# A depthwise convolution's taps: more scaled by ScalarE and summed in pairs by accumulating transfers, in buffers that attention has left

## The chip, the cores and the metric

The kernel runs on one core of one Trainium2 chip. The metric is device time in microseconds of one execution; three runs of the kernel before took 1874.3, 1874.67 and 1877.3 us. The engines are TensorE (PE, matrix products; PEld is its loading of weights), VectorE (DVE), ScalarE (ACT), GpSimd (POOL) and SyncE (SP). POOL and SP here mostly issue transfers.

## The reference

Two layers of one mixer each over a sequence of 256 with 2048 channels. One input projection feeds a convolution branch (with a depthwise causal convolution of 31 taps and a layer norm over the channels) and an attention branch of 16 heads; gates merge them.

```python
def conv_branch(a, glu, gate, conv_w, conv_b, ln_g, ln_b):
    u = a * jax.nn.sigmoid(glu)
    u = lax.conv_general_dilated(u, conv_w[:, None, :], window_strides=(1,),
        padding=[(CONV_WIDTH - 1, 0)], feature_group_count=CONV_DIM) + conv_b
    u = jax.nn.silu(layernorm(u, ln_g, ln_b))
    return u * jax.nn.silu(gate)

def hybrid_layer(...):
    proj = rmsnorm(x, norm_g) @ w_in
    ...
    y_conv = conv_branch(c_a, c_glu, c_gate, ...) @ w_proj_conv
    y_mla = mla_branch(q_down, kv_down, k_pe, m_gate, ...) @ w_proj_mla
    y = jax.nn.sigmoid(g_conv) * y_conv + jax.nn.sigmoid(g_mla) * y_mla
    return x + y @ w_out
```

## The kernel before

All large products read weights from HBM in *pieces* of 128 rows by two blocks of (mostly) 512 columns, 512 KB each, which SP loads in the order of the products, four pieces ahead, into five `raw` buffers. Precision is kept by splitting: ACT rounds a piece to `hi` (three pieces ahead, four buffers), DVE makes `lo = raw - hi` (two pieces ahead, three buffers), and PE multiplies hi by hi, lo by hi and hi by lo for both halves of the sequence: 12 matmuls a piece. The products of a layer follow in the order `glu` (the convolution's input), `down`, then for eight pairs of heads `uq`, `ukv` and more `glu` and `cgate`, then `cgate`, `mgate`, `gmla`, `pmla`, `gconv`, `pconv` (the convolution branch's projection, whose stationary operand is `ycT`, a quarter of it for each two pieces of its first block) and `wout`.

Every engine's instructions run in the order in which the program records them. That order is drawn at recording time by a planner with a clock of one *slot* a piece: `product` records a piece's splits and matmuls and then calls `background`, which records

- the steps that are due at this slot (`at_slot`), attention's above all,
- work from the queue `fill` while a budget of DVE's time for this slot lasts: taps of the convolution, then the steps of the layer norm,
- calls of `assist` while ACT's budget lasts: ACT scales a tap ahead of DVE into a `wide` buffer, at most two ahead,
- and what was put off in `late`.

The convolution is worked on for eight blocks of 256 channels (`conv(b)`): `u` holds the block's input, `v_t` its sum, and a tap is two instructions of DVE (`scalar_tensor_tensor`, one for each 128 channels), or two of ACT and one add of DVE. A block's sum goes into `s1`. After the eighth block, `layernorm` puts its steps into `fill`: the mean over channels by a matmul (`mu`), centring and squares, a second matmul (`var`), the root by steps of DVE (`rsqrt_steps`), `apply` (times the root, then silu on ACT), `gated` (times the transposed gate) and `separated` (hi by ACT and lo by DVE into `ycT`). Before the first block of `pconv`, at each second piece, `before_pconv` draws from `fill` whatever is still missing for the next quarter of `ycT`.

The profile names all these instructions by the line of one helper, L136, which records them; the tiles' names tell them apart. In the names `acc` is a product's PSUM tile, `hT` and `h_hi`, `h_lo` the normalised input, `su` and `gate` gates that are transposed by way of HBM (`turn_d`, fetched as `turned`), `qk` an attention pair's queries and keys.

Work2's two `qk` buffers, of 1536 numbers a partition, belong to the pairs of heads in turn; behind the last pair one of them becomes `ln_stats`.

Of the kernel before, what the change touches and what calls it, by code (L numbers as in the profile page):

```python
# [25 lines left out]
CONV_W = 31  # L26
PAD = CONV_W - 1
# [8 lines left out]
NPAIR = N_HEADS // 2  # L36
# [4 lines left out]
EPS = 1e-6  # L41
# [83 lines left out]
def trunk(ctx: ExitStack, tc: tile.TileContext, xT, x, g_in, pos, win, wuq, wukv, wpc, wpm, wo, cst, rows, invf, out):  # L125
# [114 lines left out]


    steps, clock, late, early = [], [0], [], []
    fill, budget, marks, owed, assist = deque(), {"vec": 0.0, "act": 0.0}, {}, [], []
# [331 lines left out]
    for l in range(DEPTH):  # L575
# [199 lines left out]
        def attention(b, pair_of=pair_of, ss_d=ss_d, kpe=kpe, ccq=ccq, ssq_t=ssq_t, gqk=gqk, A=A):  # L775
# [95 lines left out]
            def maxima():  # L871
                s0, s1 = st["s"]
                sx = work.tile([P, 2, P], F32, tag="sx", name="sx")
                act.copy(sx, s0[:, :, 1, :])
# [48 lines left out]
            def outputs():  # L923
                o = A.o_sb[:, 2 * b : 2 * b + 2, :]
                act.copy(o, st["o"][:, :, 0, :])
                late.append(lambda: vec.tensor_add(o, st["o"][:, :, 1, :], o))
                A.pairs.pop(b)

            def later(ahead, *args, **kw):
                at_slot(ahead + PAIR_LATER[b], *args, **kw)  # L930
# [14 lines left out]


        us, vs, keep = {}, {}, {"separated": {}}
        s1 = layer_c.tile([P, 2, SEQ], F32, tag="s1c", name="s1c")

        def glu_evac(b, t, ps, us=us):  # L950
# [13 lines left out]
            early.append(product_out)  # L964

        def conv(b, us=us, vs=vs, s1=s1, C=C):
            scaled = {}
# [5 lines left out]
            def scale(k):  # L973

                while k in scaled:
                    k += 1
                if k == CONV_W or len(scaled) == 2:
                    return False
                scaled[k] = wide_p.tile([P, 2, SEQ], F32, tag="w", name="tap")
                for j in range(2):  # L980
                    act.activation(scaled[k][:, j, :], us[b][:, j, k : k + SEQ], AF.Copy, scale=weight(k, j))
                return True

            def tap(k):

                if k == 0:
                    vs[b] = uv_p.tile([P, 2, PAD + SEQ], F32, tag="uv", name="v_t")
                u, v, costs = us[b], vs[b], (0.81, 0.0)
                if k == 0:
                    for j in range(2):  # L990
                        bias = C[:, C_CB + 2 * b + j : C_CB + 2 * b + j + 1]
                        vec.tensor_scalar(v[:, j, :SEQ], u[:, j, :SEQ], weight(k, j), bias, op0=ALU.mult, op1=ALU.add)
                elif k in scaled:
                    vec.tensor_add(v[:, :, :SEQ], v[:, :, :SEQ], scaled.pop(k))
                    costs = (0.73, 0.0)
                else:
                    for j in range(2):
                        vec.scalar_tensor_tensor(
                            v[:, j, :SEQ], u[:, j, k : k + SEQ], weight(k, j), v[:, j, :SEQ], op0=ALU.mult, op1=ALU.add
                        )  # L1000
                assist[:] = [lambda: scale(k + 1)]
                if k == CONV_W - 1:
                    mark(("s1", b))
                    assist.clear()
                    if b == 0:
                        vec.tensor_copy(s1, v[:, :, :SEQ])
                    else:
                        vec.tensor_add(s1, s1, v[:, :, :SEQ])
                    costs = (costs[0] + 0.6, costs[1])
                    us.pop(b)  # L1010
                return costs

            for k in range(CONV_W):
                fill.append((lambda k=k: tap(k), (None, 0, False)))

        def layernorm(vs=vs, s1=s1, C=C, keep=keep):
            marks.clear()
            stats = work2.tile([P, 5, SEQ], F32, tag="qk", name="ln_stats")
            mu_sb, ms, rstd = (stats[:, i] for i in range(3))
            s2 = stats[:, 3:]  # L1020
            wide = lambda a: a.unsqueeze(1).broadcast_to([P, 2, SEQ])

            st = {}

            def mean():
                st["mu"] = tp_p.tile([P, SEQ], F32, tag="tp", name="mu")
                over_channels(st["mu"])
                mark("mean")

            def centre(b):  # L1030
                if b == 0:
# [25 lines left out]

            def whole_s2():
                finish_late()
                halves(s2)  # L1060
                mark("s2")
                return 1.1, 0.0

# [8 lines left out]
                mark("var")  # L1072

            def factors():
                vec.tensor_scalar(ms, st["var"], EPS, None, op0=ALU.add)
                st["rsqrt"] = rsqrt_steps(rstd, ms)
                next(st["rsqrt"])
                return 0.9, 0.0

# [3 lines left out]

            def apply(b):
                v = vs[b][:, :, :SEQ]
                vec.tensor_mul(v, v, wide(rstd))
# [373 lines left out]
```

## Time and profile before

| | |
|---|---|
| median of three runs | 1874.67 us |
| the profiled execution, its own time | 1874.78 us |
| its span, first to last instruction | 1873.0 us |
| mean granted PE clock | 0.982 |
| the chain that ended last | PE 92%, DVE 4%, ACT 2% |
| DVE, `lo` of 128x1024, x630 | 766.0 us, 1.22 us each |
| ACT, `hi` of 128x1024, x630 | 654.6 us, 1.05 us each |
| weights by SP's queue | 59.1% of the 16 DMA engines' span |
| transfers of POOL's queue | 13.5% |

A row of a group gives the engine, the operation, what it writes and reads with sizes, how many, the busy time in us, the mean of one in ns, and the idle time of the engine just before with what ended it. A row of the order of time gives the start and the duration in us. A row of waits gives the sum in us, how many and the longest. A row of stretches gives each engine's busy time in a stretch, PE's granted clock, the share of the DMA engines and GB/s.

### The profile page before, as it was taken

To read this page: it belongs to the slowest core of one execution; us is meant where nothing else is said; L and a number is where in the kernel's file an instruction comes from. 1 tells how busy PE (TensorE), PEld (TensorE's weight loads), DVE (VectorE), ACT (ScalarE), POOL (GpSimd) and SP (SyncE) were. 2 spreads that over 40 slices of the span, in tenths; PEclk is the share of its full clock that TensorE was granted. 3 is DMA by queue.
4 is the path that set the end of the run, shared out by engine and by line. 5 is a ranking of instruction groups with operands and counts; after the bars stand their busy time and mean duration, and the time that the engine had idled before them with its cause. 6 is when DMAs were issued, how large, how long until landed. Compare 5 with 4: busy or idle time off the path is not lost.

```text
span 1873.0 us, 27021 instructions
## 1 busy us (share of the span) xinstructions
PE 1803.1 (96%) x8577; PEld 1587.0 (85%) x8577; DVE 1587.8 (85%) x2526; ACT 1295.7 (69%) x2363; POOL 492.7 (26%) x942
## 2 busy tenths in 40 slices
PE   9999999999999995599999999999999999976999
PEld 9988888888888884488899888888888888865888
DVE  6898988899999998567679999889999999875664
ACT  7678889888766764445557688898887667553442
POOL 1155555543100000022320555555431000001210
PEclk9999999999999998799999999999999999988999
DMA  9788788888766664277977888888877666753785
GB/s 331 238 272 280 259 279 266 262 265 259 241 204 202 203 214 140 95 235 258 320 266 218 270 282 266 273 260 261 273 256 244 204 203 203 215 180 108 256 271 173
DMA packets 138959, 445.04 MB, mean 238 GB/s; under 512 B 23680, under 2 KB 29312, under 8 KB 138816
## 3 DMA queue, kind: packets, MB, share of 16 engines
q1 hardware_dynamic: 105120, 359.89, 59.1%
q0 software_dynamic: 32832, 82.62, 13.5%
q8 instruction: 67, 1.10, 0.2%
q10 hardware_dynamic: 864, 0.80, 0.1%
q14 instruction: 76, 0.62, 0.1%
HBM read 399.18 MB, written 44.04 MB: 237 GB/s over the span
## 4 chain that ended last, share of the span: by engine, by line
PE 92%; DVE 4%; ACT 2%; DMA 1%; POOL 1%; issue 1%; DVEq 0%; SPq 0%; ACTq 0%; POOLq 0%
PE acc L136 90%; PE s L136 1%; DVE v_t L136 1%; PE o_ps L136 1%; DVE lo L136 1%; ACT hi L136 1%; DVE ln_stats L136 1%; POOL rsq_t L136 0%; DVE turned L136 0%; DVE rsq_t L136 0%; DMA raw<-in_win 0%; ACT ycT L136 0%; ACT L136 0%; DMA gx<-in_g 0%; POOL turn_d L136 0%
## 5 line engine op out<-in xcount | busy, mean ns | idle before, releaser
L136 ACT CAST hi<-raw 128x1024 fp32r<-128x1024 f32 (+3 forms) x682 | 695.0, 1027 | 437.6 <-PE acc L136 374.4
L136 DVE TENSOR_TENSOR lo<-raw,hi 128x1024 fp32r<-128x1024 f32 (+3 forms) x682 | 812.1, 1193 | 182.3 <-PE acc L136 143.8
L136 PE MATMUL acc<-hi,hT 128*128 128x512 f32 (+2 forms) x1728 | 401.1, 372 | 0.9 <-ACT junk L136 0.5
L136 PEld LDWEIGHTS acc<-hi,hT 128*128 128x128 f32 x1728 | 319.5, 189 | 42.3 <-ACT junk L136 1.1
L136 PE MATMUL acc<-hi,h_hi 128*128 128x512 f32 (+2 forms) x864 | 251.9, 373 | 0.4 <-ACT hi L136 0.4
L136 PE MATMUL acc<-hi,h_lo 128*128 128x512 f32 (+2 forms) x864 | 251.4, 373 | 0.0
L136 DVE SCALAR_TENSOR_TENSOR v_t<-u_t,cst,v_t 128x256 f32<-128x256 f32 x564 | 242.9, 479 | 4.5
L136 PE MATMUL acc<-lo,h_hi 128*128 128x512 f32 (+2 forms) x864 | 220.5, 372 | 0.0
L136 PE MATMUL acc<-lo,hT 128*128 128x512 f32 (+2 forms) x864 | 220.2, 372 | 0.0
L136 POOL DMA_DIRECT2D turned<-turn_d x88 | 49.2, 559 | 602.6 <-DVE v_t L136 393.3
L136 PE MATMUL acc<-hi,ycT 128*128 128x512 f32 x512 | 137.5, 414 | 51.4 <-ACT ycT L136 51.4
L136 PEld LDWEIGHTS acc<-hi,h_lo 128*128 128x128 f32 x864 | 161.9, 189 | 20.8
L136 ACT ACTIVATE tap<-u_t,cst 128x256 f32<-128x256 f32 x396 | 179.0, 499 | 0.3 <-DVE v_t L136 0.3
L136 PEld LDWEIGHTS acc<-lo,h_hi 128*128 128x128 f32 x864 | 161.0, 189 | 20.7
L136 PEld LDWEIGHTS acc<-hi,h_hi 128*128 128x128 f32 x864 | 160.7, 189 | 20.9 <-ACT hi L136 0.8
L136 PEld LDWEIGHTS acc<-lo,hT 128*128 128x128 f32 x864 | 160.8, 189 | 20.6
L136 POOL DMA_DIRECT2D turn_d<-gate x184 | 100.0, 551 | 264.2 <-DVE gate L136 162.7
L136 PEld LDWEIGHTS acc<-hi,ycT 128*128 128x128 f32 x512 | 105.7, 208 | 72.1 <-ACT ycT L136 54.5
L136 DVE TENSOR_TENSOR v_t<-v_t,tap 128x512 f32<-128x512 f32 x198 | 135.5, 685 | 1.5 <-DVE v_t L136 0.5
L136 PE MATMUL acc<-hi,oT 128*128 128x512 f32 x512 | 122.2, 379 | 0.0
L136 PE MATMUL acc<-hi,yT 128*128 128x512 f32 x512 | 122.2, 378 | 0.0
L136 PE MATMUL acc<-hi,qkc 128*128 128x512 f32 x448 | 110.4, 379 | 0.0
(176 smaller groups left out, 2222.2 us busy)
## 6 DMA issues: line engine op xcount, KB each, us to landing
raw<-in_win SPq DMA_DIRECT2D x382, 512.0 KB, 4.4
raw<-in_wpm SPq DMA_DIRECT2D x64, 512.0 KB, 4.3
raw<-in_wpc SPq DMA_DIRECT2D x64, 512.0 KB, 3.8
raw<-in_wo SPq DMA_DIRECT2D x64, 512.0 KB, 5.0
raw<-in_wukv SPq DMA_DIRECT2D x32, 512.0 KB, 4.3
turned<-turn_d POOLq DMA_DIRECT2D x56, 256.0 KB, 5.0
raw<-in_win SPq DMA_DIRECT2D x32, 384.0 KB, 4.7
raw<-in_wuq SPq DMA_DIRECT2D x24, 512.0 KB, 4.4
```

The lines of the kernel that those rows point to most:

```text
L136: ins = getattr(self.engine, name)(*a, **k)
```

## The change

Behind the last pair of heads (`outputs` of the last pair calls `more_taps`), the two `qk` buffers become six buffers of a tap each (`spare`), and ACT's rule is changed from (0.8, 0.85) to (0.4, 1.1): it may go on at a smaller rest of its budget, and each tap is charged with more. `scale` now takes taps from the far end (`todo.pop()`), DVE from the near end. While `spare` has a buffer, ACT scales a tap into it; the second of two is added onto the first by a transfer that POOL issues with an accumulating write (`dma_start(whole, tap, accum_op=add)`). Three slots on, the second buffer is free again and DVE's `step` may add the sum of both, once, to `v_t`. Without `spare` all is as before, with at most two single taps ahead. The end of a block is a step of its own. In `maxima` the second half of the queries comes first: its mask and maximum stand before the add of the first half, which waits for a copy of ACT. `ln_stats` is allocated when the mean is recorded.

```diff
+MERGED_AT = 3
+BESIDE_PAIRS, BEHIND_PAIRS = (0.8, 0.85), (0.4, 1.1)
...
-        while assist and budget["act"] > 0.8 and assist[0]():
-            budget["act"] -= 0.85
+        while assist and budget["act"] > pace[0][0] and assist[0]():
+            budget["act"] -= pace[0][1]
...
             def maxima():
...
-                vec.tensor_add(sx, s0[:, :, 0, :], sx)
-                for s, nkeys in ((sx, P), (s1, SEQ)):
-
+                for t, (s, nkeys) in ((1, (s1, SEQ)), (0, (sx, P))):
+                    if t == 0:
+                        vec.tensor_add(sx, s0[:, :, 0, :], sx)
                     vec.memset(s[:CHUNK, :, nkeys - CHUNK :], MASKED)
-                nb = small.tile([P, T, 2], F32, tag="nb", name="nb")
-                vec.tensor_reduce(nb[:, 0], sx, axis=AX.X, op=ALU.max, negate=True)
-                vec.tensor_reduce(nb[:, 1], s1, axis=AX.X, op=ALU.max, negate=True)
+                    vec.tensor_reduce(nb[:, t], s, axis=AX.X, op=ALU.max, negate=True)
...
         def conv(b, us=us, vs=vs, s1=s1, C=C):
+            todo, singles, st = deque(range(1, CONV_W)), deque(), {"first": None}
...
+            def scale():
+
+                if len(todo) < 2:
+                    return False
+                merged = bool(spare)
+                if not merged and len(singles) == 2:
+                    return False
+                k = todo.pop()
+                tap = spare.popleft() if merged else wide_p.tile([P, 2, SEQ], F32, tag="w", name="tap")
                 for j in range(2):
+                    act.activation(tap[:, j, :], us[b][:, j, k : k + SEQ], AF.Copy, scale=weight(k, j))
+                if not merged:
+                    singles.append((clock[0] + 1, tap))
+                elif st["first"] is None:
+                    st["first"] = tap
+                else:
+                    whole, st["first"] = st["first"], None
+                    late.append(lambda: gps.dma_start(whole, tap, accum_op=ALU.add))
+                    merging.append((clock[0] + MERGED_AT, b, whole))
+                    at_slot(MERGED_AT, lambda: spare.append(tap))
                 return True
...
+            def step():
+
+                if merging and merging[0][0] <= clock[0]:
+                    return add_merged()
+                if singles and (singles[0][0] <= clock[0] or not todo):
+                    return add(singles.popleft()[1])
+                if todo:
+                    k = todo.popleft()
...
+                        vec.scalar_tensor_tensor(v, us[b][:, j, k : k + SEQ], weight(k, j), v, op0=ALU.mult, op1=ALU.add)
+                    return 0.81, 0.0
...
+        def more_taps():
+            pace[0] = BEHIND_PAIRS
+            for _ in range(2):
+                a = work2.tile([P, 3, 2, SEQ], F32, tag="qk", name="taps")
+                spare.extend(a[:, i] for i in range(3))
```

How the instructions stand now is seen on three places. First DVE in the first layer, around the first quarter of `ycT`. `lo` rows split the pieces, `ln_stats` holds the mean, the squares' sum and the root, `v_t<-v_t,ln_stats` is centring and later `apply`, `v_t<-turned,v_t` is the gate. Before:

```order
L136 TENSOR_TENSOR lo_7757<-raw_7662,hi_7741 128x1024
L136 COPY ln_stats<-mu 128x256
L136 TENSOR_TENSOR v_t<-v_t,ln_stats 128x2x256 x8
...
L136 TENSOR_TENSOR v_t<-v_t,ln_stats 128x2x256 x4
L136 TENSOR_TENSOR v_t<-turned,v_t 128x2x128 x2
L136 TENSOR_TENSOR lo_7853<-raw_7683,hi_7759 128x1024
L136 TENSOR_TENSOR v_t<-turned,v_t 128x2x128 x2
L136 TENSOR_TENSOR ycT_7848<-v_t,ycT_7847 128x512 x2
...
L136 TENSOR_TENSOR lo_7901<-raw_7725,hi_7885 128x1024
L136 TENSOR_TENSOR v_t<-v_t,ln_stats 128x2x256 x2
```

And now, the same place:

```order
L139 SCALAR_TENSOR_TENSOR ln_stats<-rsq_t,ln_stats 128x256
L139 TENSOR_TENSOR v_t<-v_t,ln_stats 128x2x256
L139 TENSOR_TENSOR lo_7691<-raw_7584,hi_7671 128x1024
L139 TENSOR_TENSOR v_t<-v_t,ln_stats 128x2x256 x2
L139 TENSOR_TENSOR lo_7713<-raw_7604,hi_7693 128x1024
L139 TENSOR_TENSOR lo_7735<-raw_7627,hi_7715 128x1024
L139 TENSOR_TENSOR v_t<-v_t,ln_stats 128x2x256
L139 TENSOR_TENSOR v_t<-turned,v_t 128x2x128 x4
L139 TENSOR_TENSOR lo_7764<-raw_7652,hi_7737 128x1024
L139 TENSOR_TENSOR ycT_7759<-v_t,ycT_7758 128x512 x2
...
L139 TENSOR_TENSOR lo_7828<-raw_7717,hi_7812 128x1024
L139 TENSOR_TENSOR v_t<-v_t,ln_stats 128x2x256 x2
```

Before, everything from the mean to the root stood between two `lo` rows, ahead of the first quarter; now it is spread over the `lo` rows of 17 pieces ahead, of which the last are seen. From `lo_7828` on (two `lo` rows are left out ahead of it) the rows of the second, third and fourth quarter stand in the same places as before, from `lo_7901` on there.

Second, DVE in the second layer, where `ycT`'s quarters are made; the `lo` rows stand for the last pieces of `gconv`:

```order
L139 TENSOR_TENSOR v_t<-turned,v_t 128x2x128 x4
L139 TENSOR_TENSOR lo_16593<-raw_16487,hi_16566 128x1024
L139 TENSOR_TENSOR ycT_16588<-v_t,ycT_16587 128x512 x2
L139 TENSOR_TENSOR lo_16617<-raw_16505,hi_16595 128x1024
L139 TENSOR_TENSOR v_t<-v_t,ln_stats 128x2x256 x2
L139 TENSOR_TENSOR lo_16639<-raw_16526,hi_16619 128x1024
L139 TENSOR_TENSOR v_t<-turned,v_t 128x2x128 x4
L139 TENSOR_TENSOR lo_16671<-raw_16550,hi_16641 128x1024
L139 TENSOR_TENSOR ycT_16588<-v_t,ycT_16587 128x512 x2
```

Before, they stood as in the first layer, ten `lo` rows further down, the first quarter behind the last `lo` that could be made ahead of `pconv`.

Third, ACT in the convolution of the first layer, some 35 pieces ahead of the layer norm; `hi` rows stand for the pieces, and an `ACTIVATE` of `x2` is one tap. Before, one tap stood beside a piece:

```order
L136 CAST hi_6568<-raw_6476 128x1024
L136 ACTIVATE tap<-u_t,cst 128x256 x2
L136 CAST hi_6592<-raw_6499 128x1024
L136 ACTIVATE tap<-u_t,cst 128x256 x2
L136 CAST hi_6616<-raw_6522 128x1024
L136 ACTIVATE tap<-u_t,cst 128x256 x2
```

And now, into `taps`, the six borrowed buffers:

```order
L139 CAST hi_6572<-raw_6489 128x1024
L139 ACTIVATE taps<-u_t,cst 128x256 x4
L139 CAST hi_6598<-raw_6512 128x1024
L139 ACTIVATE taps<-u_t,cst 128x256 x2
L139 CAST hi_6622<-raw_6533 128x1024
L139 ACTIVATE taps<-u_t,cst 128x256 x2
L139 CAST hi_6647<-raw_6554 128x1024
L139 ACTIVATE taps<-u_t,cst 128x256 x4
```

Four taps now stand beside three pieces, where it was one beside each. On POOL's queue 37 rows `DMA taps<-taps 128x512` are new in the first layer and 33 in the second; they stand between the parking and fetching of gates.

More of the change, by code (lines that the diff above doesn't have):

```diff
@@ L873, in maxima @@
                 sx = work.tile([P, 2, P], F32, tag="sx", name="sx")
+                nb = small.tile([P, T, 2], F32, tag="nb", name="nb")
                 act.copy(sx, s0[:, :, 1, :])
-                vec.tensor_add(sx, s0[:, :, 0, :], sx)
-                for s, nkeys in ((sx, P), (s1, SEQ)):
+                for t, (s, nkeys) in ((1, (s1, SEQ)), (0, (sx, P))):
+                    if t == 0:
+                        vec.tensor_add(sx, s0[:, :, 0, :], sx)
                     vec.memset(s[:CHUNK, :, nkeys - CHUNK :], MASKED)
-                nb = small.tile([P, T, 2], F32, tag="nb", name="nb")
-                vec.tensor_reduce(nb[:, 0], sx, axis=AX.X, op=ALU.max, negate=True)
-                vec.tensor_reduce(nb[:, 1], s1, axis=AX.X, op=ALU.max, negate=True)
+                    vec.tensor_reduce(nb[:, t], s, axis=AX.X, op=ALU.max, negate=True)
                 vec.tensor_mul(nb, nb, st["rs"])
@@ L927, in outputs @@
                 A.pairs.pop(b)
+                if b == NPAIR - 1:
+                    more_taps()
             def later(ahead, *args, **kw):
@@ L947, in trunk @@
         us, vs, keep = {}, {}, {"separated": {}}
+        spare, merging = deque(), deque()
         s1 = layer_c.tile([P, 2, SEQ], F32, tag="s1c", name="s1c")
@@ L966, in conv @@
         def conv(b, us=us, vs=vs, s1=s1, C=C):
-            scaled = {}
+            todo, singles, st = deque(range(1, CONV_W)), deque(), {"first": None}
             def weight(k, j):
@@ L971, in weight @@
                 return C[:, at : at + 1]
[L973 to L977, printed above, removed]
-                    return False
-                scaled[k] = wide_p.tile([P, 2, SEQ], F32, tag="w", name="tap")
-                for j in range(2):
-                    act.activation(scaled[k][:, j, :], us[b][:, j, k : k + SEQ], AF.Copy, scale=weight(k, j))
-                return True
[L984 to L989, printed above, removed]
-                    for j in range(2):
[L991 to L995, printed above, removed]
-                else:
[L997 to L1011, printed above, removed]
@@ L1013, in conv @@
-            for k in range(CONV_W):
-                fill.append((lambda k=k: tap(k), (None, 0, False)))
+            def scale():
+                if len(todo) < 2:
+                    return False
+                merged = bool(spare)
[3 more added lines that the diff above has]
+                tap = spare.popleft() if merged else wide_p.tile([P, 2, SEQ], F32, tag="w", name="tap")
+                for j in range(2):
+                    act.activation(tap[:, j, :], us[b][:, j, k : k + SEQ], AF.Copy, scale=weight(k, j))
[8 more added lines that the diff above has]
+                    at_slot(MERGED_AT, lambda: spare.append(tap))
+                return True
@@ new lines, in add, with begin @@
+            def add(tap):
+                vec.tensor_add(vs[b][:, :, :SEQ], vs[b][:, :, :SEQ], tap)
+                return 0.73, 0.0
+            def begin():
+                vs[b] = uv_p.tile([P, 2, PAD + SEQ], F32, tag="uv", name="v_t")
+                for j in range(2):
+                    bias = C[:, C_CB + 2 * b + j : C_CB + 2 * b + j + 1]
+                    vec.tensor_scalar(vs[b][:, j, :SEQ], us[b][:, j, :SEQ], weight(0, j), bias, op0=ALU.mult, op1=ALU.add)
+                assist[:] = [scale]
+                return 0.81, 0.0
@@ new lines, in add_merged @@
+            def add_merged():
+                whole = merging.popleft()[2]
+                spare.append(whole)
+                return add(whole)
+            def step():
[5 more added lines that the diff above has]
+                    k = todo.popleft()
+                    for j in range(2):
+                        v = vs[b][:, j, :SEQ]
+                        vec.scalar_tensor_tensor(v, us[b][:, j, k : k + SEQ], weight(k, j), v, op0=ALU.mult, op1=ALU.add)
+                    return 0.81, 0.0
+                if merging:
+                    return add_merged()
+                if st["first"] is not None:
+                    whole, st["first"] = st["first"], None
+                    spare.append(whole)
+                    return add(whole)
+                return 0.0, 0.0
@@ new lines, in end @@
+            def end():
+                assist.clear()
+                mark(("s1", b))
+                v = vs[b][:, :, :SEQ]
+                if b == 0:
+                    vec.tensor_copy(s1, v)
+                else:
+                    vec.tensor_add(s1, s1, v)
+                us.pop(b)
+                return 0.73, 0.0
+            fill.append((begin, (None, 0, False)))
+            for _ in range(1, CONV_W):
+                fill.append((step, (None, 0, False)))
+            fill.append((end, (None, 0, False)))
@@ L1016, in layernorm @@
+        pace[0] = BESIDE_PAIRS
+        def more_taps():
[3 more added lines that the diff above has]
+                spare.extend(a[:, i] for i in range(3))
         def layernorm(vs=vs, s1=s1, C=C, keep=keep):
             marks.clear()
-            stats = work2.tile([P, 5, SEQ], F32, tag="qk", name="ln_stats")
-            mu_sb, ms, rstd = (stats[:, i] for i in range(3))
-            s2 = stats[:, 3:]
@@ L1025, in mean @@
             def mean():
+                st["stats"] = work2.tile([P, 5, SEQ], F32, tag="qk", name="ln_stats")
                 st["mu"] = tp_p.tile([P, SEQ], F32, tag="tp", name="mu")
@@ L1030, in centre @@
             def centre(b):
+                mu_sb, s2 = st["stats"][:, 0], st["stats"][:, 3:]
                 if b == 0:
@@ L1059, in whole_s2 @@
                 finish_late()
-                halves(s2)
+                halves(st["stats"][:, 3:])
                 mark("s2")
@@ L1074, in factors @@
             def factors():
-                vec.tensor_scalar(ms, st["var"], EPS, None, op0=ALU.add)
-                st["rsqrt"] = rsqrt_steps(rstd, ms)
+                vec.tensor_scalar(st["stats"][:, 1], st["var"], EPS, None, op0=ALU.add)
+                st["rsqrt"] = rsqrt_steps(st["stats"][:, 2], st["stats"][:, 1])
                 next(st["rsqrt"])
@@ L1085, in apply @@
                 v = vs[b][:, :, :SEQ]
-                vec.tensor_mul(v, v, wide(rstd))
+                vec.tensor_mul(v, v, wide(st["stats"][:, 2]))
                 def silu():
```

2 lines of the change are left out of this document (1 added, 1 removed).

## The prediction

> **What bounds the kernel now.** I read the page's first two parts first: how busy each engine is, and where in the span TensorE (PE) is not.
>
> ```profile
> span 1873.0 us, 27021 instructions
> PE 1803.1 (96%) x8577; PEld 1587.0 (85%) x8577; DVE 1587.8 (85%) x2526; ACT 1295.7 (69%) x2363; POOL 492.7 (26%) x942
> PE   9999999999999995599999999999999999976999
> PEclk9999999999999998799999999999999999988999
> ```
>
> PE is busy everywhere but in two places, slices 16 and 17 and slices 37 and 38, one in each layer, and there its granted clock is low too. Next the waits, those of PE alone:
>
> ```profile
> PE acc L136 <- ACT ycT L136: 51.4, 8, 11.6
> PE var L136 <- DVE parts L136: 12.8, 1, 12.8
> ```
>
> Both are the layer norm of the convolution branch: PE has run out of gate products and waits for `ycT`, the normalised and gated convolution, before `pconv`. PE's other waits on that list are small. So only what shortens these two places, or makes PE wait in new ones, moves the end. The busy time by stretches shows what runs ahead of them:
>
> ```profile
> core 0: us, PE busy (x) PEld busy (x) DVE busy (x) ACT busy (x) POOL busy (x), PEclk, DMA share, GB/s
> 500.00:725.00 225.00, 225.00 (x1044) 197.04 (x1043) 216.99 (x326) 151.45 (x228) 2.18 (x4) 1.00 0.64 208
> 725.00:750.00 25.00, 4.52 (x20) 3.45 (x18) 20.86 (x38) 8.78 (x14) 1.09 (x2) 0.68 0.20 57
> ```
>
> Ahead of the hole VectorE (DVE) is busy 216.99 of 225 us, ScalarE (ACT) 151.45. DVE is full with convolution taps, so the layer norm starts only when PE has nothing left. Now what the two places cost. The order of time of PE around them:
>
> ```profile
> 728.08 0.40 PE L136 MATMUL mu<-parts,ones 128*128 128x256 f32 x2
> 741.28 1.04 PE L136 MATMUL var<-parts,ones 128*128 128x256 f32 x2 [12.80 <-DVE parts L136]
> 753.94 3.78 PE L136 MATMUL acc<-hi,ycT 128*128 128x512 f32 x8 [11.61 <-ACT ycT L136]
> 765.85 3.78 PE L136 MATMUL acc<-hi,ycT 128*128 128x512 f32 x8 [4.59 <-ACT ycT L136]
> 779.81 3.78 PE L136 MATMUL acc<-hi,ycT 128*128 128x512 f32 x8 [5.78 <-ACT ycT L136]
> 792.42 3.40 PE L136 MATMUL acc<-hi,ycT 128*128 128x512 f32 x8 [4.58 <-ACT ycT L136]
> 804.29 1.89 PE L136 MATMUL acc<-hi,ycT 128*128 128x512 f32 x8
> 806.88 1.89 PE L136 MATMUL acc<-hi,ycT 128*128 128x512 f32 x8
> ...
> 1667.15 0.59 PE L136 MATMUL acc<-lo,hT 128*128 128x512 f32 x2
> 1677.67 3.78 PE L136 MATMUL acc<-hi,ycT 128*128 128x512 f32 x8 [9.93 <-ACT ycT L136]
> 1729.22 1.89 PE L136 MATMUL acc<-hi,ycT 128*128 128x512 f32 x8
> ```
>
> and how many products of `ycT` lie in them:
>
> ```profile
> 753.90:804.25 50.35, 35.36 (x120) 28.50 (x121) 5.17 (x8) 3.90 (x7) 0.79 0.30 100
> 1677.60:1729.18 51.58, 36.56 (x120) 29.30 (x121) 5.17 (x8) 3.94 (x8) 0.78 0.30 97
> ```
>
> At full rate a piece of 12 matmuls takes 806.88 - 804.29 = 2.59 us, 0.216 us each, so 120 take 25.9 us. First layer: from the end of `mu` at 728.48 to 804.29 are 75.8 us; less 25.9, and 0.2 for the two `var` matmuls, **49.7 us are lost**. Second layer: from 1667.58 (1667.15 and two pitches of 0.216) to 1729.22 are 61.6 us; less 25.9, **35.7 us are lost**. Together 85.4 us: the most that the change can save.
>
> **The change, part by part.** *Fewer adds on DVE.* The number of taps that ACT scales (198) and that DVE multiplies itself (282) stays. But 70 pairs of scaled taps, 37 in the first layer and 33 in the second, are summed by a transfer, so DVE adds 128 times in place of 198.
>
> ```profile
> L136 DVE SCALAR_TENSOR_TENSOR v_t<-u_t,cst,v_t 128x256 f32<-128x256 f32 x564 | 242.9, 479 | 4.5
> L136 DVE TENSOR_TENSOR v_t<-v_t,tap 128x512 f32<-128x512 f32 x198 | 135.5, 685 | 1.5 <-DVE v_t L136 0.5
> ```
>
> 70 adds at 0.685 us are 48 us, 25 us in the first layer. Not one of them is on PE's path; they matter since a piece leaves DVE little room:
>
> ```profile
> 565.37 1.22 DVE L136 TENSOR_TENSOR lo<-raw,hi 128x1024 fp32r<-128x1024 f32 x1
> 566.51 1.67 DVE L136 SCALAR_TENSOR_TENSOR v_t<-u_t,cst,v_t 128x256 f32<-128x256 f32 x4
> 568.09 1.22 DVE L136 TENSOR_TENSOR lo<-raw,hi 128x1024 fp32r<-128x1024 f32 x1
> ```
>
> The split of a piece (`lo`) occupies 566.51 - 565.37 = 1.14 us of its 2.59, so 1.45 us are left for taps, and 25 us are 17 pieces. The order confirms it: the last tap on DVE stands 18 `lo` rows earlier in the first layer (257th in place of 275th) and 17 earlier in the second. On PE, where nothing else is moved, `mu` goes up by 18 and 17 pieces, `var` by only 7 in the first layer, from piece 276 to 269, and by 17 in the second.
>
> *Second layer.* The first rows of `ycT` stand on DVE ten `lo` rows before the place where `pconv` asks for them, the last ones five. One `lo` row is one piece, 2.59 us, so five are 13 us, against waits of 4.6 to 9.9 us. All of it then lies beside gate products, and I count the whole 35.7 us.
>
> *First layer, first quarter of* `ycT`*.* From the `var` matmuls after piece 269, PE has 7 more pieces, 18.1 us, before `pconv`. In the order DVE has in that time 12 operations of the statistics and the root, 4 multiplications by it, 4 by the gate and 6 `lo`. The chain of before prices them:
>
> ```profile
> 1667.26 0.44 DVE rsq_t L136
> 1667.71 0.43 DVE rsq_t L136
> ...
> 762.58 2.56 DVE v_t L136 x6
> 765.20 0.61 ACT ycT L136
> 765.85 8.19 PE acc L136 x24
> 779.81 8.04 PE acc L136 x24
> ```
>
> 12 at a pitch of 0.45 us are 5.4; the six of 2.56 us are two by the root and four by the gate, so two more by the root bring at most 1.4; six `lo` are 6.9. With ACT's 0.6 us at the end that makes 16.9 us against 18.1. ACT is tighter:
>
> ```profile
> 763.22 2.08 ACT L136 ACTIVATE v_t<-v_t,cst 128x256 f32<-128x256 f32 x4 [0.44 <-DVE v_t L136]
> ```
>
> It may split a piece (1 us) only when PE has freed a buffer, which for the last one ahead of the cast is at 15.6 us; behind it stand the silu of one block, two of these four rows, 1 us, and the cast of 0.6. That ends 18.2 to 18.7 us after `var`. I take a wait of 0.6 us; the bounds are 0 and 4.6 us, the nearest wait in the rows.
>
> *First layer, the other three quarters.* Their rows stand where they stood: the program draws them only when `pconv` reaches them. So the waits of 4.59, 5.78 and 4.58 us stay, 15.0 us. The clock falls in such waits: 24 matmuls took 8.19 and 8.04 us in place of 5.18, and the last stretch, 792.42 to 804.29, 11.87 us for 48 matmuls in place of 10.37; 7.4 us more. The first quarter now runs on a clock that has not fallen. Still lost: 0.6 + 15.0 + 7.4 = 23.0 us; **saved: 49.7 - 23.0 = 26.7 us.** If the clock didn't fall, 34.1.
>
> *The accumulating transfers* are the unknown; no row shows one. Their wait is new: DVE's add waits for the landing, and behind it on DVE stand the next `lo`, for which PE waits. POOL waits for ACT's second scaling, and behind it stand the parking and fetching of gates. ACT waits for one of six buffers, and behind it stand the `hi` splits.
>
> ```profile
> 590.15 1.05 ACT L136 CAST hi<-raw 128x1024 fp32r<-128x1024 f32 x1 [0.73 <-PE acc L136]
> 591.10 0.90 ACT L136 ACTIVATE tap<-u_t,cst 128x256 f32<-128x256 f32 x2
> ```
>
> ```profile
> raw<-in_win SPq DMA_DIRECT2D x50, 512.0 KB, 4.3
> turned<-turn_d POOLq DMA_DIRECT2D x4, 256.0 KB, 4.2
> ```
>
> ACT splits in 0.95 us (591.10 - 590.15) and scales a tap in 0.9, so the second of two is done 2.7 us into a piece; DVE's add is placed three pieces on, behind a `lo`: 3 x 2.59 + 1.14 = 8.9 us. The transfer has 6.2 us. A plain one of the same 256 KB, issued by POOL in this stretch (500 to 725 us), lands after 4.2 us; twice that, 8.4 us, is my other bound, as the destination has to be read too. I take a value near the row, 4 to 6 us: no wait. At 8.4 us DVE would come 2.2 us late. That isn't paid 70 times: the landing hangs on ACT, not on DVE, so a DVE that is late once is late enough for all that follow, and `lo` is made two pieces ahead, with about 4 us of slack.
>
> On the 16 DMA engines 0.64 of the time is taken at 208 GB/s, so 256 KB are 0.8 us of all of them. There is one merge in 5.7 us (37 in 82 pieces, 33 in 71): 0.14 more if it costs the same, 0.28 if double.
>
> ```profile
> 375.00:400.00 25.00, 25.00 (x120) 21.95 (x119) 24.28 (x37) 19.59 (x33) 14.80 (x28) 1.00 0.92 306
> ```
>
> At a share of 0.92 PE waited for nothing, so I count nothing.
>
> *Maxima, and the buffers.*
>
> ```profile
> DVE sx L136 <- ACT sx L136: 21.3, 15, 3.4
> ```
>
> The second half's maximum is now taken while ACT copies the first half; DVE waited 21.3 us for that copy in 15 places, all beside products. PE waits for none of it: 0, and as much if it went wrong by as much. The borrowed buffers are the last pairs' own, dead by then: 0.
>
> **Sum.** The profiled execution's own time is 1874.78 us, its span of 1873.0 and 1.8 around it, 0.1 above the median of the three runs. 1874.8 - 35.7 - 26.7 = **1812.4 us**.
>
> **Rivals.** *A, late landings.* Behind a transfer of 8 to 10 us six buffers hold three merges, each for an estimated 14.4 us (two scalings, landing, waiting its turn, add): one in 4.8 us, while ACT's densest pattern in the order, four taps in three pieces, wants one in 3.9. ACT then stops, its `hi` come late and PE waits. 0.9 us on up to half of the 70 is up to 31 us: 1815 to 1843, say 1827. For it: no row shows such a transfer beside a DVE that is full. Against it: POOL's plain ones took 4.2 us there and SP's 4.3, with DVE busy 96%. The Trainium skill (SBUF — State Buffer, section SBUF: two separate sides) says that a transfer of POOL's queue stalls while DVE, in some of its modes, holds the port that both use, 620 ns becoming some 3100. By that rule this rival would be the likely one; the rows of 4.2 and 4.3 us don't bear it out.
>
> *B, slower than before.* The accumulating packets hold the DMA engines so long that weights come late. The share is 0.64 and E/5.7, for E us of all 16 engines per merge; PE is stretched from where that passes 1, at E = 2.05, and over the 153 pieces (396 us) the 62.4 us are used up at E = 2.95, 3.6 times a plain transfer. At four times, 3.24 us, the share is 1.21: 83 us lost, 1895 us. Against it: reading one more side is two times, not four.
>
> *C, the first layer gains nothing.* It has only a piece or so of room; if DVE comes to `var` a few us late, as it is full up to there, the first quarter's wait and its slow clock come back: 1874.8 - 35.7 = 1839 us. Against it: four `lo` rows with nothing between them stand behind the last taps, with some 4 us in which DVE catches up.
>
> *D, more is saved.* The clock holds through the three waits, 1805 us, or they shrink as well; with no loss at all 1789.
>
> **How the numbers follow.** Forecast, 1803 to 1822: 0.70. A beyond that, 1822 to 1843: 0.10. B, from E = 2.9: 0.10. C: 0.04. D below 1803: 0.06. The range of 1803 to 1838 leaves out B, D and the upper end of A and C, some 0.19. A measurement can tell 0.2%, 3.7 us, from no change. Of B 0.02 falls within that and 0.08 beyond it, slower; the rest, 0.90, is faster.
>
> **What would show it.** Right: no wait of PE over 2 us in the second layer; in the first, three waits of about 4.6, 5.8 and 4.6 us, and `mu` at about 728.1 - 18 x 2.59 = 681.5 us; landings of the transfers at 4 to 6 us. Wrong: waits of PE for `hi` or `lo` between 450 and 690 us (A if DVE or ACT waits for landings, B if weights land late), or a first wait near 11 us in the first layer (C).

## The result, and the profile after

The changed kernel takes 1811.9 us, median of four runs (1811.43 to 1812.45), against 1874.83 before: a ratio of 0.9662, 95% interval 0.9645 to 0.9679. The profiled execution took 1811.92 us, 62.9 less than the 1874.78 of before. The page's first parts, of the changed kernel:

```profile
span 1810.1 us, 27037 instructions
PE 1789.5 (99%) x8577; PEld 1578.9 (87%) x8577; DVE 1539.7 (85%) x2456; ACT 1293.2 (71%) x2364; POOL 556.8 (31%) x1012
PE   9999999999999999699999999999999999999999
PEclk9999999999999999899999999999999999999999
```

One of the two places where PE stood still is gone, slices 36 and 37 (the prediction miscounts them as 37 and 38), and the other is down to one slice. DVE has 70 instructions fewer and 48.1 us less (1587.8 - 1539.7). PE's waits in the changed kernel:

```profile
PE acc L139 <- ACT ycT L139: 15.0, 3, 5.8
PE acc L139 <- DVE su L139: 0.7, 2, 0.5
PE acc L139 <- ACT hi L139: 0.2, 1, 0.2
```

The wait for `var` has left the list, and of eight waits for `ycT` three are left. The order of time of PE in the changed kernel, first layer, then second:

```profile
681.66 0.40 PE L139 MATMUL mu<-parts,ones 128*128 128x256 f32 x2
710.39 0.41 PE L139 MATMUL var<-parts,ones 128*128 128x256 f32 x2
728.76 1.89 PE L139 MATMUL acc<-hi,ycT 128*128 128x512 f32 x8
738.70 3.78 PE L139 MATMUL acc<-hi,ycT 128*128 128x512 f32 x8 [4.59 <-ACT ycT L139]
752.60 3.78 PE L139 MATMUL acc<-hi,ycT 128*128 128x512 f32 x8 [5.78 <-ACT ycT L139]
765.18 3.39 PE L139 MATMUL acc<-hi,ycT 128*128 128x512 f32 x8 [4.58 <-ACT ycT L139]
777.03 1.89 PE L139 MATMUL acc<-hi,ycT 128*128 128x512 f32 x8
...
1593.81 0.40 PE L139 MATMUL var<-parts,ones 128*128 128x256 f32 x2
1640.67 1.89 PE L139 MATMUL acc<-hi,ycT 128*128 128x512 f32 x8
```

`mu` stands at 681.66 us, and nothing waits at 728.76 or 1640.67. From 728.76 to 777.03 are 48.3 us for 120 matmuls, which take 25.9 at full rate: 22.4 us are still lost, all in the first layer, 15.0 of them in the three waits and the rest on a slow clock behind them (granted clock 0.82 over these 48.3 us). Gained are 49.7 - 22.4 = 27.3 us in the first layer and 35.7 in the second, 63.0 together.

The transfers, which no row of before showed. DMA issues of the changed kernel (count, size, median us from issue to landing), and the row of its waits in which DVE stands still for them:

```profile
raw<-in_win SPq DMA_DIRECT2D x382, 512.0 KB, 4.6
taps<-taps POOLq DMA_DIRECT2D x70, 256.0 KB, 6.8
```

```profile
DVE v_t L139 <- DMA taps<-taps: 7.6, 7, 2.0
```

They land after 6.8 us (4.7 to 8.1), later than I had forecast, yet DVE waits for 7 of 70, 7.6 us in all. Busy time in 500 to 690 us, ahead of the layer norm, of before and of the changed kernel (PE, PEld, DVE, ACT, POOL, granted clock, share of the DMA engines, GB/s):

```profile
500.00:690.00 190.00, 190.00 (x882) 166.39 (x881) 184.59 (x276) 132.49 (x202) 1.09 (x2) 1.00 0.63 204
```

```profile
500.00:690.00 190.00, 190.00 (x883) 166.41 (x882) 180.01 (x278) 135.91 (x213) 27.80 (x34) 1.00 0.90 251
```

PE is busy throughout in both, but the DMA engines went from 0.63 to 0.90.

### The profile page after: what moved, and what is told of

Read it like the earlier page. It is cut to its first block, busy times and chain, and to the rows that moved or that the text cites. A ratio compares the mean times of both kernels' runs of the same rounds, so it can differ in the third digit from the quotient of the medians.

```text
span 1810.1 us, 27037 instructions
## 1 busy us (share of the span) xinstructions
PE 1789.5 (99%) x8577; PEld 1578.9 (87%) x8577; DVE 1539.7 (85%) x2456; ACT 1293.2 (71%) x2364; POOL 556.8 (31%) x1012
## 3 DMA queue, kind: packets, MB, share of 16 engines
q1 hardware_dynamic: 105120, 359.89, 60.7%
q0 software_dynamic: 42912, 100.98, 19.8%
## 4 chain that ended last, share of the span: by engine, by line
PE 93%; DVE 2%; DMA 2%; ACT 1%; issue 1%; POOL 1%; DVEq 0%; SPq 0%; ACTq 0%; POOLq 0%
PE acc L139 91%; PE s L139 2%; PE o_ps L139 1%; DVE lo L139 1%; DVE v_t L139 1%; ACT hi L139 0%; DMA turn_d<-down 0%; DMA raw<-in_win 0%; DMA down<-turn_d 0%; POOL turn_d L139 0%; POOL rsq_t L139 0%; DMA turned<-turn_d 0%; DMA gx<-in_g 0%; ACT pr L139 0%; ACT L139 0%
## 5 line engine op out<-in xcount | busy, mean ns | idle before, releaser
L139 PEld LDWEIGHTS acc<-hi,h_lo 128*128 128x128 f32 x864 | 161.9, 189 | 20.7
L139 PEld LDWEIGHTS acc<-lo,h_hi 128*128 128x128 f32 x864 | 161.0, 189 | 20.7
L139 POOL DMA_DIRECT2D taps<-taps x70 | 61.3, 876 | 283.0 <-ACT taps L139 204.2
L139 PE MATMUL acc<-hi,ycT 128*128 128x512 f32 x512 | 127.6, 391 | 15.0 <-ACT ycT L139 15.0
L139 PEld LDWEIGHTS acc<-hi,ycT 128*128 128x128 f32 x512 | 99.9, 196 | 31.2 <-ACT ycT L139 16.2
L139 ACT ACTIVATE taps<-u_t,cst 128x256 f32<-128x256 f32 x286 | 125.9, 498 | 0.8 <-DVE v_t L139 0.8
```

What stands on the lines that cost most here:

```text
L139: ins = getattr(self.engine, name)(*a, **k)
```

## The experiments

My theory: the whole gain comes from 70 adds fewer on DVE, which brings the layer norm 17 or 18 pieces forward; the transfers are hidden, the maxima are worth nothing, and what is left in the first layer is only that three quarters of `ycT` are drawn late. Rivals: the maxima or ACT's new rule carry part of it; late landings or full DMA engines cost something that the sum hides.

### The maxima alone

In the kernel before:

```diff
-for s, nkeys in ((sx, P), (s1, SEQ)):
+for t, (s, nkeys) in ((1, (s1, SEQ)), (0, (sx, P))):
+    if t == 0:
+        vec.tensor_add(sx, s0[:, :, 0, :], sx)
...
+    vec.tensor_reduce(nb[:, t], s, axis=AX.X, op=ALU.max, negate=True)
```

> The kernel before with the reordered maxima alone. My theory: the 21.3 us that DVE waited for ACT's copy shrink to a few us, all of it beside products, PE's list of waits stays (51.4 us for ycT, 12.8 for var): 1874.8 us, within 0.2%. Rival (the maxima carry a part of the gain, DVE has that time for the convolution): some of the 21.3 us reach the layer norm, 1853 to 1868 us.

1875.06 us, ratio 0.9996 (0.9987 to 1.0005). DVE's waits of this run:

```profile
DVE sx L136 <- ACT sx L136: 3.6, 2, 2.1
```

The wait fell from 21.3 to 3.6 us, and none of it reached the end. DVE's wait, in 15 places, was worth nothing, since PE was not waiting for DVE there.

### ACT's rule without the sums

```diff
 if b == NPAIR - 1:
-    more_taps()
+    pace[0] = BEHIND_PAIRS
```

> The changed kernel without the six buffers: ACT follows its new rule and scales 237 taps in place of 198, but each is added by DVE alone (237 adds, 243 taps multiplied), and no transfer accumulates. My theory: a tap given to ACT saves DVE only 0.79 - 0.71 = 0.08 us, 39 of them 3 us; in the order the layer norm stands one piece earlier: 2.6 us a layer at most, 1869 to 1875 us. Rival (ACT's new rule, not the sums by transfers, frees DVE): a good part of the gain stays, below 1850 us.

1872.11 us, ratio 0.9985 (0.9975 to 0.9995). PE's waits of this run:

```profile
PE acc L139 <- ACT ycT L139: 49.9, 8, 11.6
PE var L139 <- DVE parts L139: 11.2, 1, 11.2
```

ACT scaled 39 taps more, and the waits of 51.4 and 12.8 us shrank by 1.5 and 1.6. A tap taken over by ACT hardly relieves DVE, since its add (0.71 us from its start to the next instruction's) costs nearly as much there as the two multiplications (0.79). What relieves DVE is that a sum by a transfer leaves one add for two taps. The rival falls.

### One layer at a time

```diff
-if b == NPAIR - 1:
+if b == NPAIR - 1 and l == 0:
     more_taps()
```

(`l == 1` for the other.)

> The changed kernel with the buffers lent in the first layer alone (37 transfers). My theory, the two layers are worth what their waits were: 49.7 us less the 22.4 that stay: 1874.8 - 27.3 = 1847.5 us; PE's waits in the second layer as before (9.9 us first). Rival (the transfers cost something that the sum of both hides): 1850 us or more.

> The changed kernel with the buffers lent in the second layer alone (33 transfers). My theory: 1874.8 - 35.7 = 1839.1 us, PE's waits in the first layer as before (12.8, 11.6, 4.6, 5.8, 4.6). Rival: 1842 us or more.

First layer alone 1848.45 us (ratio 0.9853, 0.984 to 0.9867), second alone 1841.15 (0.9814, 0.9801 to 0.9828). Against the 1874.92 of before in the same comparison they save 26.5 and 33.8 us; I had 27.3 and 35.7. The first lies below the rival's 1850; the second lies between my 1839.1 and the rival's 1842. PE's waits divide as expected: with the first layer alone 39.8 us for `ycT` are left, with the second alone 26.6 and the 12.8 for `var`. The sum of 60.3 is 2.6 less than the changed kernel saves, about what the two intervals (some 2.5 us to either side) leave open: no cost of more than that is hidden in the sum.

### How late a transfer may land

```diff
-MERGED_AT = 3
+MERGED_AT = 2
```

(and `MERGED_AT = 1`)

> DVE adds a sum two pieces after ACT's second scaling in place of three: the transfer has 2 x 2.59 + 1.14 - 2.7 = 3.6 us, against a measured landing of 6.8. My theory: DVE comes some 3 us late at its first adds and then stays as late, since landings hang on ACT; lo is made two pieces (5.2 us) ahead, so PE waits for nothing new: 1811 to 1815 us. Rival (each late landing is paid): 3 us on many of the 70, 1850 us or more.

> The same with one piece: 1.0 us for the transfer. From the piece on whose end ACT waits, by hi and tap 2.7, landing 6.8, add 0.7, lo 1.2 make 11.4 us to PE; there are 4 to 4.4 pieces, 10.4 to 11.4 us. My theory: a loop through PE now, 0 to 1 us for a merge: 1815 to 1850 us, DVE's waits for landings above 100 us. Rival (lateness is paid once whatever the landing): within 0.2% of 1811.9.

With two pieces 1814.9 us (0.9684, 0.967 to 0.9699), with one 1847.43 (0.9857, 0.9841 to 0.9873). Waits with two pieces, of DVE and of PE:

```profile
DVE v_t L139 <- DMA taps<-taps: 14.4, 13, 2.9
PE acc L139 <- DVE lo L139: 0.5, 1, 0.5
```

and with one:

```profile
DVE v_t L139 <- DMA taps<-taps: 50.3, 33, 4.4
PE acc L139 <- DVE lo L139: 22.7, 25, 3.1
```

With two pieces DVE waits twice as often and PE hardly: `lo` is made far enough ahead to take 2.9 us. The median is 3.0 us above the changed kernel's, and the two intervals overlap; PE's own waits don't account for it, but its loading of weights waits for `lo` 3.2 us in nine places and in none in the changed kernel. With one, DVE's waits reach PE 25 times (the planner, which counts the slots, makes 72 transfers there in place of 70). Of the 35.5 us over the changed kernel 22.7 are in these rows; the page has 12.8 us more of busy time for the same 8577 matmuls (1802.3 for 1789.5), which is about the rest, and why these took longer stays open. The time is at the upper end of my bracket, DVE's waits are half of what I wrote (50 for over 100); I read this as PE's lateness putting off ACT's next taps and giving transfers time. So a late landing is not paid once and for all; somewhere between two pieces and one a loop through PE closes. The change, at three, stands one to two pieces from that edge.

### What accumulating costs

```diff
-gps.dma_start(whole, tap, accum_op=ALU.add)
+gps.dma_start(whole, tap)
```

> The transfers copy in place of accumulating (70 taps' sums are left out of the result: the second tap replaces the first). My theory: reading the destination is what makes the landing 6.8 us and the engines' share 0.90; plain it lands after about 4.2 us, the share in the convolution falls to about 0.77, the time stays at 1812. Rival (it is two SBUF sides, or DVE, that make it slow): landing and share stay.

1813.7 us (0.967, 0.9654 to 0.9686): the time stays. DMA issues and the stretch of 500 to 690 us of this run:

```profile
taps<-taps POOLq DMA_DIRECT2D x70, 256.0 KB, 4.8
```

```profile
500.00:690.00 190.00, 190.00 (x883) 166.41 (x882) 180.57 (x277) 134.97 (x212) 18.57 (x34) 1.00 0.78 250
```

Landing falls from 6.8 to 4.8 us and the share from 0.90 to 0.78, at the same GB/s, near the 4.2 and 0.77 that I expected; the rival, by which both would have stayed, falls. The price of one transfer comes from the pages' rows of POOL's queue (packets, MB, share of 16 engines), of the changed kernel and of this run:

```profile
q0 software_dynamic: 42912, 100.98, 19.8%
```

```profile
q0 software_dynamic: 38432, 100.98, 16.5%
```

With the spans and the 13.5% of 1873.0 us of before: (358.4 - 252.9) / 70 = **1.51 us of all 16 engines** for an accumulating transfer, and (299.0 - 252.9) / 70 = 0.66 for a plain one, if the queue's other transfers cost what they did before. The stretch, with 31 of them in 190 us, gives 1.65 and 0.92 by its shares of 0.63, 0.90 and 0.78, where the weights' packets may have taken longer too; so accumulating costs about double. The packets say the same: 144 for an accumulating transfer, (42912 - 32832) / 70 with the 32832 of before, and 80 for a plain one. Bytes are counted once in both. DVE is as full in both, so the part of 2 us is the accumulation and the load that it brings, and 4.8 us are left that a plain transfer takes here anyway. What in the accumulation takes the time, reading the destination or adding, the run doesn't show.

### More load on the DMA engines

```diff
 gps.dma_start(whole, tap, accum_op=ALU.add)
+for n in range(2):
+    spill = turn_d.tile([P, 2, SEQ], F32, tag="spill", name="spill")
+    gps.dma_start(spill, tap)
```

(recorded in `late`; in the second run `spill` is 128 x 512 and the source `x[n, :, 0:512]`)

> With each accumulating transfer POOL issues two more plain ones of its tap, 256 KB each, to HBM, which nobody reads. The share of 0.90 rises by 1.6 us in 5.7: to 1.18. Theory (a full set of DMA engines stretches PE, rival B's mechanism): 0.18 of some 400 us, 1860 to 1890 us, PE waiting for hi and lo, ACT for weights. Rival (weights come first, only landings get late): below 1840 us.

> As the run with two more transfers for each merge, but they copy 256 KB from the input x in HBM to HBM, so that no buffer of ACT waits for them; they load the DMA engines alone. Theory (the load of the engines makes weights late, and that PE waits for): ACT's waits for raw stay above those of the changed kernel (24 us), 1825 to 1850 us. Rival (the 26.8 us of that run came from ACT's waits for its tap buffers, 32.6 us there): 1811 to 1818 us.

Copies of the tap: 1838.66 us (0.9806, 0.9789 to 0.9823), 21 us below my range and just inside the rival's, with single runs on both sides of its 1840. The rival's picture, weights on time, did not hold either: ACT waited 81.0 us for weights (`in_win` and `in_wpm`). In that run ACT also waited 32.6 us for a tap buffer that the extra copy still read. So the second run loads the engines without touching ACT's buffers: 1852.9 us (0.9871, 0.985 to 0.9891), 41 us over the changed kernel and 2.9 above the upper end of my range. Waits of ACT, of PE and of DVE in the second run, and its chain that ended last, by shares of the span:

```profile
ACT hi L139 <- DMA raw<-in_win: 62.7, 45, 4.0
ACT hi L139 <- DMA raw<-in_wpm: 48.6, 36, 3.8
```

```profile
PE acc L139 <- DVE lo L139: 27.2, 22, 2.4
```

```profile
DVE v_t L139 <- DMA taps<-taps: 56.4, 28, 5.4
```

```profile
PE acc L139 74%; DMA taps<-taps 5%; DVE lo L139 2%; DVE v_t L139 2%; DMA turned<-turn_d 2%; DMA spill<-in_x 2%; PE s L139 2%; DMA raw<-in_wpm 1%; DMA raw<-in_win 1%; PE o_ps L139 1%; ACT hi L139 1%; ACT taps L139 1%; DMA turn_d<-gate 0%; DVE turned L139 0%; POOL rsq_t L139 0%
```

ACT waits 111 us for weights where the changed kernel's list has 14.8 for `in_win` and none for `in_wpm`. The load alone makes weights late; the buffers are not needed for it. But late weights look like the smaller part of the 41 us: DVE's waits for landings grew from 7.6 to 56.4 us (the median landing is 9.0 us), its waits for `hi` only from 18.6 to 20.7, and on the chain that ended last the landings of the sums stand for 5% of the span and the weights for 1% and 1%. By these rows the extra load brings rival A's late landings first and rival B's late weights beside them; how many of the 41 us fall to each stays open. This load lies 1.4 us of 16 engines a merge further on: (24.6% x 1853.7 - 358.4) / 70. By the prediction's rule for B the share of 0.90 + 1.4 / 5.7 = 1.15 would have cost 0.15 x 396 = 59 us; 41 were measured. The copies also read and write HBM, and the run doesn't separate that from the load on the engines.

### Towards the 22.4 us that are left

Three versions, each with the quarters of `ycT` earlier in the order: more sums by transfers; nearer steps of the layer norm; and a mixture.

```diff
-BESIDE_PAIRS, BEHIND_PAIRS = (0.8, 0.85), (0.4, 1.1)
+BESIDE_PAIRS, BEHIND_PAIRS = (0.8, 0.85), (0.0, 0.8)
```

> ACT's rule behind the pairs is (0.0, 0.8): 90 pairs summed by transfers in the planner's two layers, about one in 4.1 us in the first. The order has the quarters of ycT in the first layer at lo rows 273, 278, 282 and 284, needed at 281, 283, 285 and 287: three to eight rows of 2.59 us ahead. Theory (only the quarters' lateness is left to gain): no wait for ycT, 1812 - 22.4 = 1789.5 us. Rival (DMA engines full: 0.62 and 1.55/4.1 make 1.0, landings late): waits of PE for lo and hi give it back, 1795 to 1815 us.

```diff
-if after and clock[0] < marks.get(after, 1 << 30) + slots or scalar and budget["act"] < 0:
+if after and clock[0] < marks.get(after, 1 << 30) + slots:
...
-then(mean, after="s1", slots=3)
+then(mean, after="s1", slots=1)
...
-then(var, after="s2", slots=2)
+then(var, after="s2", slots=1)
```

> The transfers and taps of the changed kernel as they are; in the layer norm the mean and the variance are drawn one slot behind their sums in place of three and two, and apply doesn't wait for ACT's budget. Quarters at lo rows 277, 280, 283, 286: 10.4, 7.8, 5.2 and 2.6 us ahead of the places where they were drawn. Theory: of the waits of 4.6, 5.8 and 4.6 us 0.6 and 2.0 stay, and some 1 to 2 us of slow clock: 1793 to 1796 us. Rival (mean and variance now come before DVE's sums are done, ACT's silu before its splits): PE waits for parts or hi take it back, above 1800 us.

```diff
-BESIDE_PAIRS, BEHIND_PAIRS = (0.8, 0.85), (0.4, 1.1)
+BESIDE_PAIRS, BEHIND_PAIRS = (0.8, 0.85), (0.4, 0.85)
...
-then(mean, after="s1", slots=3)
+then(mean, after="s1", slots=2)
```

(and the other two lines of the version above)

> Steps of the layer norm nearer (mean two slots behind its sum, variance one, apply without ACT's budget) and ACT's rule (0.4, 0.85), 75 pairs summed by transfers. Quarters at lo rows 275, 278, 281 and 284, needed at 281, 283, 285 and 287. Theory: no wait for ycT: 1789 to 1791 us; DMA share in the convolution about 0.95. Rival (share this high makes lo or hi late): 1795 us or more.

More sums: 1807.95 us (0.9643, 0.9629 to 0.9658). Nearer steps: **1790.06 us** (0.9548, 0.9532 to 0.9564). The mixture: 1791.03 (0.9555, 0.954 to 0.9569), the upper end of what I expected and no gain over nearer steps alone. With more sums, the rival's range held and my 1789.5 did not; PE's first wait, and ACT's for the six buffers, are:

```profile
PE acc L139 <- DVE lo L139: 10.3, 13, 2.4
```

```profile
ACT taps L139 <- DVE v_t L139: 26.5, 10, 6.0
ACT taps L139 <- DMA taps<-taps: 14.9, 10, 4.9
```

The waits for `ycT` are gone there too, but 87 transfers give back 18 of the 22.4 us, 10.3 of it in the row for `lo`. ACT waits 41 us for a buffer, 0.8 in the changed kernel, with landings up to 12.0 us and a share of 0.90 to 0.97: six buffers no longer hold what is under way. That is rival A's mechanism more than late weights: ACT's waits for weights (`in_win`, `in_wo`, `in_wpm`) grew too, from 23.8 to 48.5 us, but on the chain that ended last landings of sums stand for 7% of the span and no weights for as much as 1%. With nearer steps instead, the page and PE's waits read:

```profile
span 1788.3 us, 27036 instructions
PE 1781.8 (100%) x8577; PEld 1573.5 (88%) x8577; DVE 1538.6 (86%) x2456; ACT 1291.7 (72%) x2364; POOL 556.9 (31%) x1012
PE   9999999999999999999999999999999999999999
PEclk9999999999999999999999999999999999999999
```

```profile
PE acc L139 <- ACT hi L139: 0.9, 1, 0.9
PE acc L139 <- DVE ycT L139: 0.3, 1, 0.3
```

One wait of 0.3 us is left of the layer norm. Same transfers, same taps; only three limits of the planner are changed, and it beats both kernels: 1.2% faster than the changed one, and 1811.9 - 22.4 = 1789.5 us was the most to be had by ending these waits. I had counted 0.6 and 2.0 us of waits and some slow clock, 1793 to 1796; it came out better. ACT's casts of the four quarters in this run:

```profile
719.31 1.14 ACT L139 CAST ycT<-v_t 128x512 fp32r<-128x512 f32 x2
726.71 1.13 ACT L139 CAST ycT<-v_t 128x512 fp32r<-128x512 f32 x2
736.59 1.14 ACT L139 CAST ycT<-v_t 128x512 fp32r<-128x512 f32 x2
743.33 1.14 ACT L139 CAST ycT<-v_t 128x512 fp32r<-128x512 f32 x2 [1.03 <-DVE v_t L139]
```

PE's first products of the quarters stand at 728.96, 734.14, 739.32 and 744.50 us, so the casts end 8.5, 6.3 and 1.6 us ahead of them and the last one just in time. I take it that what was drawn earlier for the first quarters also cleared the work that the later ones stood behind; this was not tried by itself.

## Why the prediction was right

- **DVE's relief, and how far it moves the layer norm.** 70 adds of 0.685 us are 48 us; DVE's busy time fell by 48.1. `mu` was to stand at 681.5 us and stands at 681.66. The run without the sums shows that they, not ACT's rule, do it: 2.8 us are saved without them.
- **Second layer, 35.7 us.** No wait there in the changed kernel; 33.8 with that layer alone.
- **First layer, first quarter.** I took a wait of 0.6 us out of 0 to 4.6; it is 0. It was close, as the order of time of ACT in the changed kernel shows:

```profile
727.51 1.12 ACT L139 CAST ycT<-v_t 128x512 fp32r<-128x512 f32 x2
```

The cast ends at 728.63, 0.1 us before PE's first product of `ycT` at 728.76. 0.6 us is the whole difference between 1812.4 and what my terms give without it, 1811.8.
- **First layer, the other quarters.** 4.59, 5.78 and 4.58 us to the hundredth, as their rows stand where they stood, and the clock falls behind them as before: 22.4 us. Rival D (a clock that holds) did not come, though the waits could be removed, as the last runs show.
- **The accumulating transfers.** The conclusion held, the step to it did not. I put the landing at 4 to 6 us, by the 4.2 of four plain transfers from HBM, and DVE's turn 6.2 us behind ACT; the landing took 6.8, outside the sign that I had named, and by these two numbers most adds would have come late. But the room was mis-sized as well. POOL's issue and DVE's add of the same sum, in the changed kernel:

```profile
520.79 0.86 POOL L139 DMA_DIRECT2D taps<-taps  x1 [10.26 <-ACT taps L139]
530.34 0.86 POOL L139 DMA_DIRECT2D taps<-taps  x1 [8.68 <-ACT taps L139]
```

```profile
527.92 0.69 DVE L139 TENSOR_TENSOR v_t<-v_t,taps 128x512 f32<-128x512 f32 x1
538.15 0.69 DVE L139 TENSOR_TENSOR v_t<-v_t,taps 128x512 f32<-128x512 f32 x1
```

They lie 7.1 and 7.8 us apart. Two errors of about a us cancelled, which was luck; the margin in these two was 0.3 and 1 us, and the lead of `lo` covered the 7 that missed it. The run with two pieces shows that cover at work.
- **DMA engines.** A share of 0.14 to 0.28 more was expected, 0.27 came. The double price was the right one: 1.51 us against my 0.8 for a plain one (measured here: 0.66).
- **Maxima.** 0, as counted.
- **The rivals.** A did not come: with landings of 6.8 us DVE's waits never reached PE; with `MERGED_AT = 1` they did. The rule of the Trainium skill named there (SBUF — State Buffer, section SBUF: two separate sides) is for DVE in some of its modes; making A the likely outcome by it took it for any full DVE. The trace does not show the stall for this mix, mostly `tensor_tensor` and `scalar_tensor_tensor`: plain transfers from SBUF to SBUF landed after 4.8 us with DVE busy 180.57 of 190 us. A is also what the version with 87 transfers runs into. B did not come; with 1.4 us more per merge weights do come late, and even that, with the landings that it delays, costs 41 of the 63 us. C, a first wait near 11 us, did not come: there was no first wait, though ACT's cast had 0.1 us to spare.

## What to carry to other kernels

An engine that runs full beside the bound one costs nothing until its last result is due: count how many pieces earlier that result stands in the order, and the gain is the wait at that place and the slow clock behind it, no more. Giving half of an operation to another engine helped here only as far as it removed an instruction from the full one, the second add; then check what the new path loads, since DMA engines at a share of 0.90 had room for little else (17 more sums gave back 18 us). And before adding more relief, look at the limits that the program itself sets: three slots of waiting in the planner and a condition on ACT's budget, taken out together, were worth 21.8 us that more transfers could not bring.

## What the runs showed of the hardware that I had not expected

An accumulating transfer of 256 KB within SBUF takes 1.51 us of all 16 engines against 0.66 for the plain one (2.3 times by the queue's rows, 1.8 by the stretch), 144 packets against 80, 2 us longer to land, and 0.87 us of POOL to issue in place of 0.55, while the page's bytes and GB/s count it once: the share of time, not GB/s, showed that the engines were nearly full. And a sum of shares above 1 overstated the cost here: 1.15 by sum cost two thirds of what it said, and there the packets of SP's queue took less time in all (58.3% of 1853.7 us, against 60.7% of 1810.1).
